# An fp32 two-block transformer on one core: the first block of each feed-forward stage as eight plain products, post-norms spread over two stages

## The chip, the cores and the metric

One NeuronCore of a Trainium2 chip runs the whole program. The time is device microseconds of one execution. All tensors are fp32; batch 1, 512 tokens, width 1024.

## What is computed

Two blocks, each with two layers, on `x` of 512 x 1024. Cut to what matters here:

```python
# first block, per layer: h = h + mixer(rms(h)); h = h + swiglu(rms(h))
def swiglu(h, wg, wu, wd):
    return (silu(h @ wg) * (h @ wu)) @ wd            # 1024 -> 2816 -> 1024
# layer 0's mixer: gated linear attention + stick-breaking attention
# layer 1's mixer: conformer convolution (1024 -> 2048, gate, 31 taps, layer norm, 1024 -> 1024)

# second block, per layer: x = x + rms(mixer(rms(x)), post); x = x + rms(mlp(rms(x)), post)
def sq_relu_mlp(x, w_up, w_down):
    return square(relu(x @ w_up)) @ w_down            # 1024 -> 4096 -> 1024
# layer 0's mixer: differential attention;  layer 1's: short gated convolution (1024 -> 3072, 3 taps)
```

So there are four feed-forward stages: two gated ones (swiglu) and two MLPs. In the second block every mixer and every MLP ends in a post-norm: its whole output must be squared and summed before it can be scaled and added to the residual.

## The kernel before, in words

The residual `res` is held transposed, eight tiles of 128 features x 512 tokens. Every matrix product is made of three fp32r matmuls (`mm3`, lines 296 to 299): each operand is split into a high part (ScalarE copy to fp32r) and a remainder (VectorE subtraction). For weights `w_parts` (L267 to L274) does that: a ScalarE copy into `wh`, a VectorE subtraction at L273 into `wl`; there are four buffers of each, of 128 x 1024. Raw weights come over SyncE's queue into three buffers of 1 MB. For the residual `split_x` (L389) does it, with VectorE at L391. A row scale, one over the root mean square, is applied after the products, because it is a factor per token: `bc_rstd` (L380) squares the eight residual tiles on ScalarE, adds five on GpSimd and three on VectorE (both L373), sums over features by two fp32 matmuls with a tile of ones (L383, L384) and takes Ln and Exp on ScalarE.

The up-projections of the feed-forward stages (`group_s`, L451) compute blocks of 512 output columns with seven products of half-size matrices in place of eight: the features, the columns and the tokens are each cut in two, and a product is 24 matmuls of 256 tokens (L468 to L472). For that it needs sums of weight quarters (VectorE, L480, L492, L493, L507), sums of products (L498, L501, L505), and sums of the activations: for the first four feature tiles the difference of the two token halves (`split_s3`, L413), written over the second half of `xh` and `xl`, and for each pair of tiles three sum tiles (`split_sums`, L420 to L428) in `ph_so`. There are 38 such blocks: 11 in each gated stage and 8 in each MLP. In the first block of a stage one product is put earlier (`first`).

The down-projection and the other projections are plain (`group`, L303, and `out_proj`, L751): four PSUM banks of 128 features x 512 tokens, two passes of 512 features each. Where a post-norm follows, the last weight chunk of the second pass is run in two token halves, and `after_half` is called behind each of them. `Post` (L970) does the post-norm: `evac_last` (L987) takes a finished tile out of PSUM (in the MLP by two VectorE operations, L993 and L994, in the attention by a ScalarE copy), squares it on ScalarE and adds it up on GpSimd (L984). `half` (L1013) makes the matmul with ones (L1016), Ln and Exp, and then `apply` for the tiles: a VectorE scale (L1006), an add to the residual on GpSimd for the tiles 0 to 3 and on VectorE for the others (both L1007), the split, and at a feed-forward stage the differences and sums. Behind it the next stage begins with its `bc_rstd`. At the end of the program `store` transposes the residual back (L1283), copies it out of PSUM (L1285) and writes it (L1286), token half by token half.

What sets the order of instructions on each engine is a scheduler that runs while the program is built. It goes by program order among what is ready, by its own estimate of the times; on the chip every engine follows that order. Two kinds of PSUM tile have four banks each: `mm` for the projections, `at` for the rest.

Of the kernel before, what the change touches and what calls it, by code (L numbers as in the profile page):

```python
# [17 lines left out]
P = 128  # L18
# [91 lines left out]
def body(ctx: ExitStack, tc: tile.TileContext, A, out, consts):  # L110
# [192 lines left out]
    def group(chunks, outs, hs, ls, evac, k_outer=False, halves=(), after_half=None):  # L303
# [6 lines left out]
        for ci, ch in enumerate(chunks):  # L310
# [3 lines left out]
            for tr in trs:  # L314
                ix = [(o, k) for k in range(nk) for o in range(len(outs))] if k_outer else [
                    (o, k) for o in range(len(outs)) for k in range(nk)]
                for o, k in ix:
                    c, m = outs[o]
                    mm3(pss[o][:m, tr], wh[k][:, c : c + m], wl[k][:, c : c + m], hs[kk + k][:, tr], ls[kk + k][:, tr],
# [3 lines left out]
                if after_half and ci == last:  # L323
                    after_half(trs.index(tr))
            kk += nk

    def group_nat(chunks, n, hs, ls, evac, k_outer=False):
# [4 lines left out]
        for ci, ch in enumerate(chunks):  # L332
# [4 lines left out]
            for t, k in ix:  # L337
                ts_ = slice(t * P, (t + 1) * P)
                ps = pss[t][:, :n]
                pe.matmul(ps, hs[kk + k][:, ts_], wh[k], start=ci == 0 and k == 0, stop=False)  # L340
# [90 lines left out]
    def split_s(o, gname, gi):  # L431

        if o < 4:
            split_x(o, V(gname, gi * 8 + o), T0)
            split_s3(o, V(gname, gi * 8 + o))
        else:
            split_x(o, V(gname, gi * 8 + o))
            split_sums(o - 4, V(gname, gi * 8 + o - 4), V(gname, gi * 8 + o))

    def split_s_half(k, gname, gi, i):  # L440

        g = V(gname, gi * 8 + k)
        if i == 0 or k >= 4:
            split_x(k, g, HALVES[i])
        if i == 1:
            if k < 4:
                split_s3(k, g)
            else:
                split_sums(k - 4, V(gname, gi * 8 + k - 4), g)

    def group_s(w0, w1, evac, first=False):  # L451


        bb = []
        for kh in range(2):
# [6 lines left out]
            else:  # L462
                for n, (ap, c) in enumerate((w0, w1)):
                    sync.dma_start(rv[:, :, n * 256 : (n + 1) * 256], ap[rows, c : c + 256].rearrange("(k p) c -> p k c", p=P))
            bb += [rv[:, :, :256], rv[:, :, 256:]]
# [19 lines left out]

        if first:
            product(d, parts(b21), xs(4, T0), True)
# [11 lines left out]
        evac(1, 0, u2)  # L499
        product(a, parts(b12), xs(0, T1))  # L500
        dve.tensor_add(p5, a, p5)  # L501
        evac(1, 1, p5)
        if not first:
            product(d, parts(b21), xs(4, T0), True)
        dve.tensor_add(p1, d, p1)  # L505
        evac(0, 0, p1)
        dve.tensor_add(b21, b21, b22)  # L507
        product(a, parts(b21), xs(4, T1))
        evac(0, 1, a)
# [257 lines left out]
    def add_res_sums(gname, gi):  # L767
        def f(o, ps, tr):
            dve.tensor_add(res[o], res[o], ps)
            split_s(o, gname, gi)  # L770
        return f
# [549 lines left out]
```

## Time and profile before

| | us |
|---|---|
| median of three runs | 2486.16 (2483.38 to 2489.35) |
| the profiled execution | 2486.35 |
| its span, first to last instruction | 2484.5 |
| TensorE busy | 2362.6 |
| VectorE busy | 1620.5 |
| ScalarE busy | 1186.9 |
| GpSimd busy | 233.7 |
| mean granted TensorE clock | 0.978 |

Engines in the profile: PE is TensorE's matmuls, PEld its weight loads, DVE VectorE, ACT ScalarE, POOL GpSimd, SP SyncE. "L273" is line 273 of the kernel. An arrow names what ended a wait. PEclk is the granted TensorE clock as a share of full speed. Matmul records overlap, since the engine is pipelined; how fast it goes is read from how many stand in a stretch. The stages lie in the span, in us and roughly, as follows: attention of the first block to 302, first gated stage to 640, conformer convolution to 900, second gated stage to 1240, differential attention to 1517, first MLP to 1889, short convolution to 2089, second MLP to the end.

### The profile page before, as it was taken

What the parts mean: (1) busy time and instruction counts of PE and PEld (TensorE: products, weight loads), DVE (VectorE), ACT (ScalarE), POOL (GpSimd) and SP (SyncE); (2) the same over time, 40 slices, a digit from 0 to 9 for tenths busy, and PEclk for the clock granted to TensorE, in tenths of its full rate; (3) what the DMA queues carried; (4) which work ended last, traced back from release to release, by engine and by line L of the source; (5) the groups of instructions that cost most, each with busy time, mean ns of one, the idle gap of its engine ahead of it and who ended that gap; (6) DMA issues with size and microseconds to landing.
All of it is one profiled execution on the core that took longest, in us unless ns stands there. A gap on an engine that the chain in (4) does not pass through costs nothing. (4 is left out here: it accounts for less than half of the span.)

```text
span 2484.5 us, 33155 instructions
## 1 busy us (share of the span) xinstructions
PE 2362.6 (95%) x13550; PEld 2008.3 (81%) x13550; DVE 1620.5 (65%) x2096; ACT 1186.9 (48%) x1966; POOL 233.7 (9%) x212
## 2 busy tenths in 40 slices
PE   8999999999998799999999996999998996999997
PEld 6677788989786589898977775898897885898996
DVE  4344795858699787685746767665566545755565
ACT  4663553535654354343434555663354224653552
POOL 0000001010103100202100003000004103000002
PEclk9999999999999899999999998999999998999998
DMA  5112133332312114242331110332332231322420
GB/s 162 35 51 68 51 102 102 103 102 94 111 34 68 34 53 135 68 136 68 128 99 56 51 52 18 122 101 84 102 119 68 85 102 35 102 85 89 132 85 34
DMA packets 148105, 206.84 MB, mean 83 GB/s; under 512 B 5822, under 2 KB 88305, under 8 KB 147953
## 3 DMA queue, kind: packets, MB, share of 16 engines
q1 hardware_dynamic: 147921, 204.72, 25.6%
q8 instruction: 106, 1.74, 0.3%
q14 instruction: 46, 0.38, 0.0%
q10 hardware_dynamic: 32, 0.01, 0.0%
HBM read 202.61 MB, written 2.10 MB: 82 GB/s over the span
## 5 line engine op out<-in xcount | busy, mean ns | idle before, releaser
L297 PE MATMUL ps<-rs,wh 128*128 128x512 f32 (+1 forms) x2976 | 1028.9, 346 | 9.1 <-ACT rs L102 8.2
L298 PE MATMUL ps<-rs,wh 128*128 128x512 f32 (+1 forms) x2976 | 1028.8, 346 | 5.4 <-DVE rs L391 5.4
L299 PE MATMUL ps<-rs,wl 128*128 128x512 f32 (+1 forms) x2976 | 1024.5, 344 | 2.4 <-DVE wl L273 2.4
L273 DVE TENSOR_TENSOR wl<-wraw,wh 128x1024 fp32r<-128x1024 f32 x500 | 606.7, 1221 | 513.3 <-ACT wh L102 512.5
L102 ACT ACTIVATE wh<-wraw 128x1024 fp32r<-128x1024 f32 x500 | 519.7, 1047 | 682.7 <-PE ps L298 553.0
L297 PEld LDWEIGHTS ps<-rs,wh 128*128 128x128 f32 x2976 | 563.7, 190 | 87.1 <-ACT rs L102 11.0
L298 PEld LDWEIGHTS ps<-rs,wh 128*128 128x128 f32 x2976 | 564.1, 190 | 84.1 <-DVE rs L391 7.0
L299 PEld LDWEIGHTS ps<-rs,wl 128*128 128x128 f32 x2976 | 563.6, 189 | 76.8 <-DVE wl L273 2.8
L297 PE MATMUL ps<-ph_so,wh 128*128 128x256 f32 x912 | 260.0, 285 | 5.0 <-ACT fs L102 3.4
L299 PE MATMUL ps<-ph_so,wl 128*128 128x256 f32 x912 | 259.5, 285 | 3.6 <-DVE wl L273 2.4
L298 PE MATMUL ps<-ph_so,wh 128*128 128x256 f32 x912 | 258.6, 284 | 0.7 <-DVE ph_so L396 0.7
L102 ACT ACTIVATE fs<-fs 128x512 f32<-128x512 f32 (+2 forms) x368 | 208.5, 574 | 86.4 <-DVE fs L994 34.5
L297 PEld LDWEIGHTS ps<-ph_so,wh 128*128 128x128 f32 x912 | 175.1, 192 | 7.5 <-ACT fs L102 4.8
L299 PEld LDWEIGHTS ps<-ph_so,wl 128*128 128x128 f32 x912 | 174.9, 192 | 7.7 <-DVE wl L273 7.5
L102 ACT ACTIVATE fs<-ps 128x512 f32<-128x512 f32 (+1 forms) x207 | 116.3, 564 | 129.2 <-PE ps L299 100.5
L298 PEld LDWEIGHTS ps<-ph_so,wh 128*128 128x128 f32 x912 | 175.2, 192 | 1.7 <-DVE ph_so L396 0.9
L102 ACT ACTIVATE rs<-fs 128x512 fp32r<-128x512 f32 (+1 forms) x148 | 91.7, 623 | 78.5 <-DVE fs L800 44.1
L984 POOL TENSOR_TENSOR fs<-fs,fs 128x256 f32<-128x256 f32 (+1 forms) x44 | 46.6, 1058 | 744.4 <-ACT fs L102 737.6
L396 DVE TENSOR_TENSOR rs<-fs,rs 128x512 fp32r<-128x512 f32 x133 | 91.0, 689 | 19.2 <-ACT rs L102 18.8
L812 POOL TENSOR_TENSOR fs<-fs,fs 128x512 f32<-128x512 f32 x32 | 52.2, 1632 | 481.9 <-DVE fs L810 481.9
L102 ACT ACTIVATE rs<-fs,vec 128x256 fp32r<-128x256 f32 (+1 forms) x92 | 52.6, 587 | 67.7 <-DVE fs L814 17.0
L373 POOL TENSOR_TENSOR fs<-fs,fs 128x512 f32<-128x512 f32 x28 | 42.3, 1510 | 342.7 <-ACT fs L102 336.8
(280 smaller groups left out, 2198.6 us busy)
## 6 DMA issues: line engine op xcount, KB each, us to landing
wraw<-in_mlp_w_up_dram SPq DMA_DIRECT2D x32, 1024.0 KB
wraw<-in_mlp_w_down_dram SPq DMA_DIRECT2D x32, 1024.0 KB
wraw<-in_ffn_w_up_dram SPq DMA_DIRECT2D x44, 512.0 KB
wraw<-in_ffn_w_gate_dram SPq DMA_DIRECT2D x44, 512.0 KB
wraw<-in_ffn_w_down_dram SPq DMA_DIRECT2D x20, 1024.0 KB
wraw<-in_cv_w_pw_dram SPq DMA_DIRECT2D x16, 512.0 KB
wraw<-in_attn_w_qkv_dram SPq DMA_DIRECT2D x16, 512.0 KB
wraw<-in_conv_w_in_dram SPq DMA_DIRECT2D x16, 512.0 KB
```

The lines of the kernel that those rows point to most:

```text
L102: r = self.engine.activation(out, in_, func, **kw)
L273: dve.tensor_sub(v(wl), src, v(b(wh)))
L297: pe.matmul(ps, wh, h, start=start, stop=False, skip_group_check=True)
L298: pe.matmul(ps, wh, l, start=False, stop=False, skip_group_check=True)
L299: pe.matmul(ps, wl, h, start=False, stop=stop, skip_group_check=True)
L373: r = eng.tensor_add(acc, acc, s)
L396: dve.tensor_sub(l, src, b(h))
L812: pool_e.tensor_add(res[o], res[o], s)
L984: pool_e.tensor_add(self.acc[:, tr], self.acc[:, tr], s[:, tr])
```

## The change

Four things change.

1. The first block of each of the four feed-forward stages runs all eight block products by `group_plain`, one token half after the other: the k-tiles outside, four column tiles inside, 96 matmuls of 256 tokens for a half. It needs no sums. The tiles of sums and differences for the later blocks are made during it and after it (`split_all_sums`, then `split_s3`).
2. `Post` no longer works per half behind the projection. `steps` is called after each output tile of the second token half: after the second, the statistics of the first half and two of its tiles, then one, then five. The second half's statistics and tiles (`second`) come from within the next stage: behind k = 1 of the first half of the plain block, or of the short convolution's first group. The adds on GpSimd are those of the tiles 1, 3 and 5.
3. The short convolution's first group (`group_first`) runs wholly in token halves, where before its first weight chunk did. The row scales (`bc_rstd`) come later: in the gated stages behind k = 3 of the plain block's first half, in the MLPs behind the plain block, in the short convolution behind k = 5 of the group's second half, in the conformer convolution and the attention ahead of the last k of the first group.
4. At the end, the second half's statistics come ahead of the first half's store.

The diff, cut to its core (the signatures follow):

```diff
+    def group_first(chunks, outs, hs, ls, evac, at):
+        pss = [bank() for _ in outs]
+        ws = [load_w(*ch) for ch in chunks]
+        nk = chunks[0][2]
+        for i, tr in enumerate(HALVES):
+            for k in range(2 * nk):
+                wh, wl = (w[k % nk] for w in ws[k // nk])
+                for o, (c, m) in enumerate(outs):
+                    mm3(pss[o][:m, tr], wh[:, c : c + m], wl[:, c : c + m], hs[k][:, tr], ls[k][:, tr],
+                        i == 0 and k == 0, i == 1 and k == 2 * nk - 1)
+                if (i, k) in at:
+                    at[i, k]()
+        for o, (c, m) in enumerate(outs):
+            evac(o, pss[o][:m], None)
...
+    def group_plain(w0, w1, evac, at):
+        ws = []
+        for rv in load_blocks(w0, w1):
+            for h in range(2):
+                wh, wl = w_parts(rv[:, 2 * h : 2 * h + 2, :].rearrange("p k c -> p (k c)"), 1024)
+                ws += [(wh[:, k * T : (k + 1) * T], wl[:, k * T : (k + 1) * T]) for k in range(2)]
+        for th, tr in enumerate((T0, T1)):
+            pss = [bank(), bank()]
+            for k in range(8):
+                for n in range(2):
+                    for p in range(2):
+                        wh, wl = (t[:, n * 256 + p * P : n * 256 + (p + 1) * P] for t in ws[k])
+                        mm3(pss[n][:, p * 256 : (p + 1) * 256], wh, wl, xh[k][:, tr], xl[k][:, tr], k == 0 and p == 0, k == 7)
+                if (th, k) in at:
+                    at[th, k]()
+            for n in (1, 0):
+                evac(n, th, pss[n], False)
...
-                group_s((wu, col), (wg, col), evac, pi == 0 and fc == 0)
+                if pi == 0 and fc == 0:
+                    group_plain((wu, col), (wg, col), evac, {(0, 3): norm, (1, 0): lambda: split_all_sums("ffnn", layer)})
+                    after_first()
+                else:
+                    group_s((wu, col), (wg, col), evac)
...
+                (pool_e if k in (1, 3, 5) else dve).tensor_add(res[k][:, x], res[k][:, x], m[:, x])
...
+        def steps(self, n):
+            if n == 2:
+                self.stats(0)
+            ks = {2: range(0, 2), 3: range(2, 3), 4: range(3, 8)}.get(n)
+            if ks:
+                self.apply(ks, 0)
+
+        def second(self):
+            self.stats(1)
+            self.apply(range(8), 1)
+            self.free()
...
-                group_s((wu, f0 * P), (wu, f0 * P + 256), evac, pi == 0 and g == 0)
+                if pi == 0 and g == 0:
+                    group_plain((wu, f0 * P), (wu, f0 * P + 256), evac, {
+                        (0, 1): before.second, (1, 0): lambda: split_all_sums("fpre", layer)})
+                    for k in range(4):
+                        split_s3(k, V("fpre", layer * 8 + k))
+                    rb, acc = bc_rstd(res)
+                    freeF(acc)
+                    dve.tensor_mul(rb, rb, rb)
+                    post = Post().then("fpost", layer, nxt)
+                else:
+                    group_s((wu, f0 * P), (wu, f0 * P + 256), evac)
...
+            group_first(ch, outs, xh, xl, cv_evac, {(0, 1): post.second, (1, 5): cv_norm})
...
-    mlp(1, None, store)
+    post = mlp(1, None, post)
+    post.stats(1)
+    store(0)
+    post.apply(range(8), 1)
+    store(1)
+    post.free()
```

## Rows read from the trace of the kernel before

**Rows 1.** The page's first section: busy us, share of the span, instructions

```profile
PE 2362.6 (95%) x13550; PEld 2008.3 (81%) x13550; DVE 1620.5 (65%) x2096; ACT 1186.9 (48%) x1966; POOL 233.7 (9%) x212
```

**Rows 2.** Stretches; columns: us, busy us and instructions by engine, PEclk, DMA share, GB/s

```profile
298.00:340.00 42.00, 35.86 (x248) 32.31 (x247) 39.43 (x55) 28.47 (x43) 1.52 (x1) 0.96 0.16 51
655.00:685.00 30.00, 28.81 (x122) 22.51 (x121) 24.19 (x36) 25.58 (x61) 2.06 (x1) 1.00 0.33 106
900.00:980.00 80.00, 75.35 (x609) 72.90 (x609) 70.15 (x81) 44.55 (x59) 0.00 (x0) 1.00 0.31 99
1240.00:1260.00 20.00, 19.15 (x89) 14.88 (x88) 16.27 (x26) 11.04 (x17) 1.95 (x2) 1.00 0.35 117
1517.60:1588.40 70.80, 46.10 (x343) 42.65 (x344) 65.33 (x95) 49.50 (x85) 12.02 (x12) 0.83 0.21 69
1878.00:1926.00 48.00, 37.84 (x221) 32.45 (x220) 36.48 (x53) 21.67 (x39) 23.05 (x20) 0.89 0.21 66
2088.60:2159.60 71.00, 46.62 (x343) 43.43 (x343) 65.42 (x95) 49.41 (x85) 12.11 (x12) 0.81 0.21 67
2453.00:2484.50 31.50, 16.60 (x87) 12.24 (x85) 19.93 (x39) 6.21 (x14) 11.49 (x14) 0.70 0.18 67
1600.00:1620.00 20.00, 20.00 (x87) 16.09 (x86) 3.76 (x4) 4.65 (x7) 0.00 (x0) 1.00 0.34 106
1640.00:1660.00 20.00, 20.00 (x172) 20.00 (x171) 17.71 (x19) 15.81 (x23) 0.00 (x0) 1.00 0.33 106
1513.40:1566.00 52.60, 28.16 (x197) 24.87 (x196) 50.65 (x81) 33.39 (x65) 15.82 (x16) 0.77 0.11 37
```

**Rows 3.** Groups by line, 1513.4 to 1566: busy us, mean ns, idle before

```profile
L273 DVE TENSOR_TENSOR wl<-wraw,wh 128x1024 fp32r<-128x1024 f32 x6 | 7.3, 1218 | 1.3 <-ACT wh L102 1.3
L383 PE MATMUL ps<-fs,ones 128*128 128x512 f32 x2 | 2.1, 1142 | 18.2 <-POOL fs L373 18.2
L1016 PE MATMUL ps<-fs,ones 128*128 128x256 f32 x2 | 1.2, 714 | 4.7 <-POOL fs L984 4.7
L384 PE MATMUL ps<-fs,ones 128*128 128x512 f32 x2 | 1.1, 644 | 0.4 <-DVE fs L373 0.4
```

**Rows 4.** Timeline, 2100 to 2135, GpSimd and VectorE: start us, us

```profile
2112.95 2.79 POOL L373 TENSOR_TENSOR fs<-fs,fs 128x512 f32<-128x512 f32 x2 [1.75 <-ACT fs L102]
...
2114.55 1.48 DVE L1007 TENSOR_TENSOR fs<-fs,fs 128x256 f32<-128x256 f32 x1
...
2118.47 0.41 DVE L1007 TENSOR_TENSOR fs<-fs,fs 128x256 f32<-128x256 f32 x1
2118.80 0.48 DVE L425 SCALAR_TENSOR_TENSOR fs<-fs,vec,fs 128x256 f32<-128x256 f32 x1
2119.20 0.68 DVE L373 TENSOR_TENSOR fs<-fs,fs 128x512 f32<-128x512 f32 x1
```

**Rows 5.** Timeline, 1500 to 1592, TensorE and VectorE

```profile
1511.62 0.70 PE L1016 MATMUL ps<-fs,ones 128*128 128x256 f32 x2 [0.61 <-POOL fs L984]
...
1513.45 3.13 DVE L1006 SCALAR_TENSOR_TENSOR fs<-fs,vec,fs 128x256 f32<-128x256 f32 x4 [4.52 <-ACT fs L102]
...
1587.98 0.39 PE L297 MATMUL ps<-rs,wh 128*128 128x512 f32 x1
```

**Rows 6.** Groups by line, 1513.4 to 1566, GpSimd

```profile
L1007 POOL TENSOR_TENSOR fs<-fs,fs 128x256 f32<-128x256 f32 x8 | 7.1, 906 | 5.5 <-DVE fs L1006 5.5
L373 POOL TENSOR_TENSOR fs<-fs,fs 128x512 f32<-128x512 f32 x4 | 5.5, 1380 | 4.9 <-ACT fs L102 4.8
L984 POOL TENSOR_TENSOR fs<-fs,fs 128x256 f32<-128x256 f32 x4 | 3.3, 827 | 6.9 <-ACT fs L102 6.9
```

**Rows 7.** Timeline of the end of the span

```profile
2456.26 0.70 PE L1016 MATMUL ps<-fs,ones 128*128 128x256 f32 x2 [1.20 <-POOL fs L984]
...
2470.01 1.22 PE L1016 MATMUL ps<-fs,ones 128*128 128x256 f32 x2 [2.66 <-POOL fs L984]
2472.22 4.33 DVE L1006 SCALAR_TENSOR_TENSOR fs<-fs,vec,fs 128x256 f32<-128x256 f32 x6 [3.88 <-ACT fs L102]
```

More of the change, by code (lines that the diff above doesn't have):

```diff
@@ L301, in body, with group @@
     HALVES = (slice(0, 256), slice(256, 512))
-    def group(chunks, outs, hs, ls, evac, k_outer=False, halves=(), after_half=None):
+    def group(chunks, outs, hs, ls, evac, k_outer=False, halves=(), steps=None, late=None):
         pss = [bank() for _ in outs]
@@ L318, in group @@
                     c, m = outs[o]
+                    if late and ci == last and k == nk - 1 and o == 0:
+                        late()
                     mm3(pss[o][:m, tr], wh[k][:, c : c + m], wl[k][:, c : c + m], hs[kk + k][:, tr], ls[kk + k][:, tr],
@@ L339, in group_nat @@
                 ps = pss[t][:, :n]
+                if late and ci == last and k == nk - 1 and t == 0:
+                    late()
                 pe.matmul(ps, hs[kk + k][:, ts_], wh[k], start=ci == 0 and k == 0, stop=False)
@@ L1017, in half, with apply, free @@
             rsqrt_ln(self.rm[:, tr], pb[:, :256], 1.0 / D)
-            _, _, nxt, each = self.args
-            for k in range(4 if nxt and not self.sums else 8):
-                self.apply(k, tr)
-            if each:
-                each(i)
-        def finish(self):
-            if self.args[2] and not self.sums:
-                for k in range(4, 8):
-                    self.apply(k, slice(0, T))
+        def apply(self, ks, i):
+            gname, gi, nxt = self.args
+            x = HALVES[i]
+            for k in ks:
+                m = self.m[k]
+                dve.scalar_tensor_tensor(m[:, x], m[:, x], V(gname, gi * 8 + k), self.rm[:, x], ALU.mult, ALU.mult)
+                (pool_e if k in (1, 3, 5) else dve).tensor_add(res[k][:, x], res[k][:, x], m[:, x])
+                if nxt:
+                    split_x(k, V(nxt[0], nxt[1] * 8 + k), x)
+        def steps(self, n):
[8 more added lines that the diff above has]
+            self.free()
+        def free(self):
             freeF(self.rm, self.m, self.acc)
@@ L1055, in body @@
     dve.tensor_scalar(gsub, V("subln"), 1.0 - lam_init, None, ALU.mult)
-    rb, acc = bc_rstd(res)
-    pr = bank("at")
-    for t in range(NT):
-        for i in range(2):
-            pe.matmul(pr[:, t : t + 1], acc[i][:, t * P : (t + 1) * P], ones[:, 0:1], start=i == 0, stop=i == 1, skip_group_check=True)
     rn2 = cpool.tile([P, NT], F32, name="rn2")
-    rsqrt_ln(rn2, pr[:, :NT], 1.0 / D)
-    freeF(acc)
     sync.dma_start(*const_tiles(["dmask", "rot", "cosr", "sinr"]))
@@ L1069, in body, with da_norm @@
     cosb, sinb = C["cosr"], C["sinr"]
-    dve.tensor_mul(cosb, cosb, rb)
-    dve.tensor_mul(sinb, sinb, rb)
-    freeF(rb)
+    def da_norm():
+        rb, acc = bc_rstd(res)
+        pr = bank("at")
+        for t in range(NT):
+            for i in range(2):
+                pe.matmul(pr[:, t : t + 1], acc[i][:, t * P : (t + 1) * P], ones[:, 0:1], start=i == 0, stop=i == 1, skip_group_check=True)
+        rsqrt_ln(rn2, pr[:, :NT], 1.0 / D)
+        freeF(acc)
+        dve.tensor_mul(cosb, cosb, rb)
+        dve.tensor_mul(sinb, sinb, rb)
+        freeF(rb)
     wqkv = A["attn_w_qkv_2"][0]
@@ L1270, in body @@
     freeF(rb, rb2)
-    post = Post().then("mpost", 1, ("fpre", 1), sums=True)
+    post = Post().then("mpost", 1, ("fpre", 1))
     out_proj(A["conv_w_out_2"][0], 0, 8, hh, hl, lambda o, ps, tr: post.evac_last(o, ps, tr), halves=True,
-             after_half=post.half)
+             steps=post.steps)
     freeR(hh, hl)
-    post.finish()
     def store(i):
```

148 lines of the change are left out of this document (66 added, 82 removed).

## The prediction, before the run

> **What bounds the kernel now.** I read the page's first section, then cut the span into stretches, then asked in the bad stretches what TensorE waits for. TensorE is busy for 2362.6 of 2484.5 us [rows 1], so 122 us are idle and the rest can only be shortened by less work. The stretches [rows 2] say where the idle time lies. Inside a stage TensorE does not rest: 172 matmuls of 256 columns in 20 us (0.116 us each) and 87 of 512 columns in 20 us (0.230 us each). At the seams it does: 6.1 us idle at the first gated stage (298 to 340), 4.6 at the second (900 to 980), 24.7 and 24.4 at the two MLP stages, 10.2 at the short convolution, 14.9 at the end, 1.2 at the conformer convolution and 0.9 at the attention. That is 87 us.
>
> At an MLP seam the granted clock averages 0.83 and 0.81, so lost time is more than idle time there. Of the 70.8 us after the out-projection, the 336 matmuls of the first two blocks need 39.1 us at 0.116, and L1016, L383 and L384 4.4 [rows 3]; **27 us** are lost.
>
> What ends those waits: TensorE stands 18.2 us at L383 for GpSimd's L373, after 4.7 us at L1016 [rows 3]. GpSimd is only the last in line. VectorE is busy for 50.65 of the 52.6 us from 1513.4 on, GpSimd for 15.82 [rows 2]: the seam is a **VectorE queue** of post-norm, split, difference and sum tiles, into which L383 waits.
>
> **VectorE's prices.** Back to back, a fused operation on 256 columns starts 0.40 us before the next one, an add 0.33; each record is 0.08 longer than that, so a 512-column add (0.68) counts 0.60 [rows 4] and a weight remainder of 1024 columns (1.22) 1.14 [rows 3]. The stretch's 81 instructions are 44 fused ones, 16 adds of 256 columns, 12 of 512 and 9 of 1024: 17.6 + 5.3 + 7.2 + 10.3 = 40.4 us. The other 10.3 are delay beside GpSimd: L1007 takes 0.41 alone and 1.48 while GpSimd's L373 runs [rows 4]. So 65% of GpSimd's 15.82 us came on top.
>
> The Trainium skill, SBUF — State Buffer, "Who interferes with whom", says that a VectorE instruction with two SBUF inputs and a GpSimd instruction that reads SBUF exclude each other and the loser fully blocks. The single 1.48 us instance agrees; the stretch's 65% is below it. What it would give is a rival below.
>
> **The change, part by part.**
>
> *Eight products for seven, four times.* 192 matmuls replace 168; 24 x 0.116 = 2.8 us of TensorE each, **11.2 in all**. Nothing hides it where TensorE is the bound.
>
> *First block's VectorE work.* Seven remainders, four weight sums and three product sums become four remainders: 3 x 1.14 + 4 x 1.14 + 3 x 0.60 = 9.8 us less, two weight sums of which ran before the queue begins now.
>
> *MLP stages.* Now the first statistics matmul stands after the first half with an idle wait of 0.61, and VectorE starts at 1513.45 [rows 5]. Afterwards it stands behind two outputs of the second half (24 matmuls, 2.8 us), so VectorE starts about 1.9 us later, at 1515.3; TensorE no longer waits. From there, before the second block's two first products can run, VectorE has: first-half apply 8 x 0.40 + 5 x 0.33 + 8 x 0.40 = 8.05 (three adds go to GpSimd, four now); second half the same; two remainders 2.3; four evacuations 2.4; sums tiles 4 x (3 x 0.40 + 0.60 + 0.33) = 8.5; difference tiles 4 x 0.73 = 2.9; square adds and the squared scale 1.8; two remainders and a weight sum of the second block 3.4. Sum: 37.4. GpSimd runs 6 x 0.91 + 4 x 1.38 + 4 x 0.83 = 14.3 us [rows 6]; at 65%, 9.3. So the second block's second product starts at 1515.3 + 46.7 = 1562.0, its first could start 2.8 earlier, 1559.2. Now the second block, counted back from the first 512-column matmul at 1587.98 [rows 5] by 168 x 0.116, effectively starts at 1568.5: 9.3 us gained. If the differences and the squared scale (3.5 us, needed only later in that block) slip behind, 12.8. I take **11 per stage, 22**. TensorE's own bound would be 27 - 2.8 = 24 per stage, reached only if VectorE's queue stayed hidden; it sits nearer 11, because 37 us of work stand against 22.3 us of plain block. The low end is 4, with full exclusion. L383 now waits behind the plain block (192 matmuls, 22.3 us); its chain needs the second-half adds, ready about then, so I cost it nothing beyond VectorE's queue. If its squares come late, it holds the second block up, in the same gap.
>
> *Gated stages.* The residual is complete before the block, the splits are full width, and only four sums and differences (11.4 us) plus 4.2 of evacuation and some 7 of remainders and adds are queued beside 22.3 us of plain block. L383 stands at k = 3, 5.6 us in; the gate evacuations that need its result wait until the half ends at 11. First stage: 6.1 - 2.8 - 0.7 left over = **+2.6** (bounds -1 to +3). Second: 4.6 - 2.8 - 0.8 = **+1** (-2 to +2).
>
> *Short convolution.* 256-column pairs for one 512-column matmul cost 2 x 0.116 against 0.230, nothing to 0.3 us. VectorE's apply (16.1), remainders (2.3) and GpSimd's delay fill the 22.3 us of the first group, so the halves pace closely; then L383 at k = 5 of the second half holds what follows it, and the first evacuation waits for its Ln, Exp and square, an estimated 3 to 4 us in which the next group has no bank. Of 10.2 us some 6 remain: **+4.5** (bounds 0 and 9).
>
> *Conformer and attention.* L383 moves into the group's last step: **+1** and **+0.8**, the idle now shown. Row scales come later by a microsecond or two: the bounds are -2 each and +1.2, +0.9. The constant load on SP's queue and the two GpSimd copies behind it now precede the sums; some 22 us of group cover them.
>
> *End.* Now the second statistics matmul waits until 2470.01 for squares that ran behind output copies, and VectorE's last apply starts at 2472.22 [rows 7]. Afterwards those statistics are asked for before the stores. The first ones can run at 2456.26, when their squares are there now [rows 7]; 24 matmuls later, at 2459.5, the half ends; two adds, a square and a GpSimd add put the last square near 2462.7, and the second apply follows the first on VectorE, at about 2465.7 (an estimate). **+6.5** (bounds 3 and 9); then adds, transposes, copies and stores as now. DMA counts do not change: each first block loads two weight tiles, released earlier as no weight is rewritten.
>
> **Sum.** 22 + 2.6 + 1 + 4.5 + 1 + 0.8 + 6.5 = 38.4, which already has the 11.2 in it. The profiled execution took 2486.35 us, 0.2 over the median of 2486.16: 2486.35 - 38.4 = **2448 us**.
>
> **Rivals.**
> 1. *VectorE's queue stays hidden*, the seams go to TensorE's bound: MLP 24 each, short convolution 8: gain 68, **2418**. For it: all of that work has the whole plain block to run in. Against: 46.7 us in 22.3 of cover. 0.15.
> 2. *VectorE is held for all of GpSimd's time*: 14.3 instead of 9.3 per MLP stage takes 5 off each gain, the short convolution keeps 1, the end 3.5: 12 + 2.6 + 1 + 1 + 1.8 + 3.5 = 22, **2464**. For it: the 1.48 us instance; against: the 65%. 0.17. This is what the rule of the Trainium skill's SBUF — State Buffer would do.
> 3. *The matmuls' order does not follow*: it is settled when the program is built, so L383 could stand where it stands now, the 27 us stay and the eighth product is added: 38.4 - 22 - 5.6 = 11, **2475**. 0.05.
> 4. *Slower: the plain block holds all four weight buffers* (wh, wl) until late in its second half, and the second block's weights are converted behind evacuations and difference tiles that wait for that half's end. At the first MLP seam VectorE idles 1.3 us for such weights [rows 3]; the rival decides where each of the four stages has 38.4 / 4 = 9.6 us of added gap. At 12: 2448 + 48 = **2496**. For it: VectorE runs in a fixed order; against: two of the buffers are free from k = 3 of the second half, 5.6 us before its end. 0.08.
>
> **Numbers.** The forecast has 0.55, its own range 2437 to 2460 (MLP 8 to 15, short convolution 1 to 7). To leave out no more than 2 in 10, I reach over rivals 2 and 3, and downward to just short of rival 1: 2421 to 2478. Within 0.2% (5 us, about what a measurement of this kernel can tell from no change) lie the edges of rivals 3 and 4: 0.05. Slower: the rest of rival 4, 0.07. Faster: 0.88.
>
> **What would show it.** Right: 24 more matmuls at each of four stages; waits at L1016 near nothing; TensorE's idle at each MLP seam down to 10 to 16 us, with VectorE over 90% busy until the second block's second product; a last apply near 2435 to 2440 in a shorter span. Rival 1 shows VectorE with gaps in the plain block; rival 2 VectorE operations at 1 us and more beside each GpSimd add; rival 3 a wait of 18 us at L383 again; rival 4 TensorE idle after the last plain matmul at all four stages with the remainder waiting for its weight. A gated stage that idles more than 3 us, or L383 ending more than 5 us of wait in the short convolution, makes that term wrong.

## The result, and the profile after

The changed kernel takes 2451.18 us (median of four runs, 2448.55 to 2452.56) against 2486.49 for the kernel before beside it: a ratio of 0.9857 with an interval of 0.984 to 0.9874. It is faster by 35.3 us; 38.4 were forecast, a time of 2448. The profiled execution took 2451.22 us. The page's first section, against [rows 1], shows the 144 matmuls added (96 for four products, 48 for the short convolution's pairs) and 9.6 us more TensorE time in a span 35 us shorter:

```profile
PE 2372.2 (97%) x13694; PEld 2023.2 (83%) x13694; DVE 1587.3 (65%) x2084; ACT 1175.0 (48%) x1954; POOL 224.4 (9%) x204
```

**Where it came from.** I divided both spans at the places where TensorE changes from 512-column to 256-column matmuls or back, read from the timelines; the same places exist in every kernel here. A "seam" runs from such a change to the stage's first down-projection. Lengths in us (gains are rounded after subtracting):

| stretch | before | after | gain | forecast |
|---|---|---|---|---|
| start, to the first gated seam | 302.6 | 306.8 | -4.2 | 0 |
| first gated seam | 91.3 | 85.7 | 5.5 | 2.6 |
| from its last down-projection through the conformer convolution | 270.1 | 268.5 | 1.6 | 1 |
| second gated seam | 88.3 | 84.7 | 3.6 | 1 |
| from its last down-projection through the attention | 289.6 | 288.3 | 1.3 | 0.8 |
| first MLP seam | 84.0 | 76.4 | 7.6 | 11 |
| short convolution | 199.1 | 191.4 | 7.7 | 4.5 |
| second MLP seam | 84.2 | 76.5 | 7.8 | 11 |
| end, from the last 256-column half | 37.1 | 32.9 | 4.2 | 6.5 |

The stretches not listed (three down-projections and blocks between them in each stage) agree to 0.1 us each. Outside the start the gain is 39.3 us, so the forecast's 38.4 is nearly met, by terms that are off in both directions. The start gave 4.2 back in this pair of profiles, though up to 268 us the order of the instructions is the same in both kernels. The windows from 100 to 150 us, of before and of after (start:end, length, busy us and instructions by engine, PEclk, DMA share, GB/s):

```profile
100.00:150.00 50.00, 50.00 (x231) 34.98 (x230) 18.50 (x32) 32.83 (x65) 0.52 (x1) 0.97 0.14 43
```

```profile
100.00:150.00 50.00, 50.00 (x208) 34.31 (x208) 17.28 (x29) 29.89 (x60) 0.52 (x1) 0.90 0.13 42
```

TensorE is busy for all 50 us in both, yet gets through 208 matmuls in place of 231, at a granted clock of 0.90 in place of 0.97. Over the twelve profiles of this study the start lasts from 299.8 to 306.8 us; the last experiment below, with the changed kernel's own order on every engine, has 303.3. The kernel before varies as well: beside the first two sets of experiments it took 2488.87 and 2489.71 us. So single runs are read by their stretches, not by their totals. Of the variants below, the first was run four times and the parts put together five times; the others were run once. Where a variant leaves the MLP seams as they are, these take 76.4 to 77.2 us, so less than 1 us in one seam is no finding.

**The seams after**, answering to [rows 2] in its order, each window moved with its stage: the two gated stages, the first MLP, the short convolution, the second MLP, the end. The seventh is 20 us inside the first MLP's seam; the eighth is the gap in it.

```profile
302.20:344.20 42.00, 41.44 (x319) 39.22 (x318) 35.93 (x53) 27.59 (x43) 1.30 (x1) 1.00 0.20 62
897.10:977.10 80.00, 79.78 (x661) 78.37 (x661) 69.53 (x86) 46.41 (x62) 0.00 (x0) 1.00 0.31 99
1509.80:1572.80 63.00, 49.50 (x366) 46.20 (x367) 58.86 (x92) 43.66 (x79) 12.63 (x10) 0.86 0.18 59
1862.60:1910.60 48.00, 43.30 (x302) 39.37 (x301) 45.31 (x77) 23.60 (x44) 17.42 (x19) 0.96 0.21 67
2065.50:2128.80 63.30, 50.11 (x366) 46.81 (x367) 59.12 (x93) 43.80 (x79) 12.81 (x10) 0.87 0.18 59
2422.10:2449.40 27.30, 16.88 (x87) 12.87 (x85) 20.93 (x41) 6.33 (x14) 9.56 (x12) 0.69 0.21 77
1520.00:1540.00 20.00, 15.48 (x132) 15.27 (x131) 20.00 (x39) 15.09 (x32) 8.86 (x7) 0.95 0.17 53
1535.20:1549.90 14.70, 3.46 (x8) 1.17 (x6) 14.22 (x21) 9.60 (x19) 5.55 (x4) 0.60 0.00 0
```

The gated stages hardly idle any more (0.6 and 0.2 us). Each MLP seam idles 13.5 and 13.2 us where it idled 24.7 and 24.4. VectorE is busy for all of the 20 us from 1520 on, which reach 4.8 us into the gap, and for 14.22 of 14.70 us in the gap.

What stands where L383 stood 18.2 us in [rows 3]: the row scale's two matmuls with ones are now L406 and L407, and the square adds L396. Groups by line, 1509.8 to 1572.8 (busy us, mean ns, idle before and its releaser):

```profile
L396 POOL TENSOR_TENSOR fs<-fs,fs 128x512 f32<-128x512 f32 x4 | 7.2, 1791 | 7.6 <-ACT fs L102 7.4
...
L406 PE MATMUL ps<-fs,ones 128*128 128x512 f32 x2 | 2.1, 1142 | 5.6 <-POOL fs L396 5.6
L407 PE MATMUL ps<-fs,ones 128*128 128x512 f32 x2 | 2.1, 1142 | 5.7 <-DVE fs L396 5.7
```

The gap in the timeline of TensorE: the plain block's last matmul, the two waits, the first matmuls of the second block's first and second products.

```profile
1535.20 0.28 PE L299 MATMUL ps<-rs,wl 128*128 128x256 f32 x1
1541.04 2.08 PE L406 MATMUL ps<-fs,ones 128*128 128x512 f32 x2 [5.56 <-POOL fs L396]
1548.79 2.08 PE L407 MATMUL ps<-fs,ones 128*128 128x512 f32 x2 [5.68 <-DVE fs L396]
1549.88 1.20 PE L297 MATMUL ps<-rs,wh 128*128 128x256 f32 x1
...
1553.97 0.28 PE L297 MATMUL ps<-ph_so,wh 128*128 128x256 f32 x1
```

What VectorE and GpSimd do meanwhile, from the timeline of all engines:

```profile
1533.59 7.40 POOL L396 TENSOR_TENSOR fs<-fs,fs 128x512 f32<-128x512 f32 x4 [7.38 <-ACT fs L102]
1533.96 0.48 DVE L447 SCALAR_TENSOR_TENSOR fs<-fs,vec,fs 128x256 f32<-128x256 f32 x1
1534.35 1.02 DVE L419 TENSOR_TENSOR ph_so<-fs,ph_so 128x512 fp32r<-128x512 f32 x2
1535.29 1.50 DVE L448 SCALAR_TENSOR_TENSOR fs<-fs,vec,fs 128x256 f32<-128x256 f32 x1
1536.71 1.75 DVE L419 TENSOR_TENSOR ph_so<-fs,ph_so 128x512 fp32r<-128x512 f32 x1
...
1538.38 1.48 DVE L446 SCALAR_TENSOR_TENSOR fs<-fs,vec,fs 128x256 f32<-128x256 f32 x1
1539.79 1.48 DVE L419 TENSOR_TENSOR ph_so<-fs,ph_so 128x256 fp32r<-128x256 f32 x1
...
1541.59 0.47 DVE L440 SCALAR_TENSOR_TENSOR rs<-fs,vec,rs 128x256 fp32r<-128x256 f32 x1
...
1547.25 1.49 DVE L396 TENSOR_TENSOR fs<-fs,fs 128x512 f32<-128x512 f32 x2 [0.27 <-ACT fs L102]
1548.72 1.22 DVE L273 TENSOR_TENSOR wl<-wraw,wh 128x1024 fp32r<-128x1024 f32 x1
```

While GpSimd's four adds run, four VectorE instructions take 1.50, 1.75, 1.48 and 1.48 where 0.48, 0.68, 0.48 and 0.41 are the usual durations: 4.2 us lost. The row of 7.40 us merges four adds, which singly last 2.92, 1.33, 1.59 and 1.32 us: in the first 1.8 us of the long one VectorE's instructions keep their usual durations, and from then on theirs are the long ones. The differences (L440) for the later blocks stand ahead of VectorE's share of the square adds (L396), and the second block's first weights (L273) stand behind all of it.

The end, against [rows 7]: both statistics matmuls (now L1047), VectorE's output copies (L1349) and the start of the second apply (L1055).

```profile
2425.38 0.70 PE L1047 MATMUL ps<-fs,ones 128*128 128x256 f32 x2
...
2433.48 1.22 PE L1047 MATMUL ps<-fs,ones 128*128 128x256 f32 x2 [0.39 <-POOL fs L1026]
```

```profile
2435.23 0.74 DVE L1056 TENSOR_TENSOR fs<-fs,fs 128x256 f32<-128x256 f32 x2
2435.90 1.27 DVE L1349 COPY fs<-ps 128x512 f32<-128x512 f32 x2
2437.10 0.86 DVE L1055 SCALAR_TENSOR_TENSOR fs<-fs,vec,fs 128x256 f32<-128x256 f32 x2
```

### The profile page after: what moved, and what is told of

Read it like the earlier page. It is cut to its first block, busy times and chain, and to the rows that moved or that the text cites. A ratio compares the mean times of both kernels' runs of the same rounds, so it can differ in the third digit from the quotient of the medians.

```text
span 2449.4 us, 33423 instructions
## 1 busy us (share of the span) xinstructions
PE 2372.2 (97%) x13694; PEld 2023.2 (83%) x13694; DVE 1587.3 (65%) x2084; ACT 1175.0 (48%) x1954; POOL 224.4 (9%) x204
## 3 DMA queue, kind: packets, MB, share of 16 engines
q8 instruction: 107, 1.75, 0.3%
## 5 line engine op out<-in xcount | busy, mean ns | idle before, releaser
L297 PE MATMUL ps<-rs,wh 128*128 128x512 f32 (+1 forms) x3120 | 1069.1, 343 | 12.3 <-ACT rs L102 10.7
L298 PE MATMUL ps<-rs,wh 128*128 128x512 f32 (+1 forms) x3120 | 1066.1, 342 | 5.5 <-DVE rs L414 5.5
L299 PE MATMUL ps<-rs,wl 128*128 128x512 f32 (+1 forms) x3120 | 1064.9, 341 | 2.3 <-DVE wl L273 2.3
L273 DVE TENSOR_TENSOR wl<-wraw,wh 128x1024 fp32r<-128x1024 f32 (+1 forms) x488 | 591.5, 1219 | 507.7 <-ACT wh L102 506.9
L102 ACT ACTIVATE wh<-wraw 128x1024 fp32r<-128x1024 f32 (+1 forms) x488 | 508.4, 1047 | 685.1 <-PE ps L298 546.8
L297 PEld LDWEIGHTS ps<-rs,wh 128*128 128x128 f32 x3120 | 591.5, 190 | 89.6 <-ACT rs L102 13.1
L298 PEld LDWEIGHTS ps<-rs,wh 128*128 128x128 f32 x3120 | 592.5, 190 | 82.5 <-DVE rs L414 6.8
L299 PEld LDWEIGHTS ps<-rs,wl 128*128 128x128 f32 x3120 | 592.2, 190 | 75.0 <-DVE wl L273 2.7
L299 PE MATMUL ps<-ph_so,wl 128*128 128x256 f32 x816 | 232.2, 285 | 1.5
L297 PE MATMUL ps<-ph_so,wh 128*128 128x256 f32 x816 | 231.0, 283 | 1.7 <-ACT wh L102 1.7
L298 PE MATMUL ps<-ph_so,wh 128*128 128x256 f32 x816 | 230.7, 283 | 0.0
L299 PEld LDWEIGHTS ps<-ph_so,wl 128*128 128x128 f32 x816 | 156.3, 192 | 4.3 <-DVE wl L273 4.3
L297 PEld LDWEIGHTS ps<-ph_so,wh 128*128 128x128 f32 x816 | 156.4, 192 | 2.5 <-ACT wh L102 2.1
L298 PEld LDWEIGHTS ps<-ph_so,wh 128*128 128x128 f32 x816 | 156.3, 192 | 0.0
L1026 POOL TENSOR_TENSOR fs<-fs,fs 128x256 f32<-128x256 f32 (+1 forms) x44 | 42.9, 976 | 708.0 <-ACT fs L102 700.9
L396 POOL TENSOR_TENSOR fs<-fs,fs 128x512 f32<-128x512 f32 x28 | 43.9, 1568 | 348.1 <-ACT fs L102 335.9
```

The costliest lines, as they stand in the source:

```text
L102: r = self.engine.activation(out, in_, func, **kw)
L273: dve.tensor_sub(v(wl), src, v(b(wh)))
L297: pe.matmul(ps, wh, h, start=start, stop=False, skip_group_check=True)
L298: pe.matmul(ps, wh, l, start=False, stop=False, skip_group_check=True)
L299: pe.matmul(ps, wl, h, start=False, stop=stop, skip_group_check=True)
L396: r = eng.tensor_add(acc, acc, s)
```

## The experiments

My theory of the changed kernel: an MLP seam is still held by the order in which the row scale is asked for. Its square adds and its two matmuls with ones stand ahead of the second block's products, though its result is needed only later. Rivals: VectorE simply has too much work for the cover it is given; or GpSimd's adds hold VectorE up. Every edit is against the changed kernel. Stretches are named as in the table above; lengths in us:

| kernel | start | 1st gated | 2nd gated | 1st MLP | its first down-projection | short conv. | 2nd MLP | end |
|---|---|---|---|---|---|---|---|---|
| changed kernel | 306.8 | 85.7 | 84.7 | 76.4 | 45.0 | 191.4 | 76.5 | 32.9 |
| scale late | 306.3 | 86.0 | 85.0 | 77.0 | 46.3 | 191.5 | 75.2 | 32.9 |
| scale late, tied | 305.1 | 85.9 | 84.9 | 70.1 | 46.3 | 191.5 | 70.2 | 32.9 |
| squares on VectorE | 305.2 | 85.5 | 84.7 | 75.0 | 45.0 | 191.5 | 74.3 | 32.9 |
| post-norm adds on VectorE | 302.5 | 85.7 | 84.7 | 75.6 | 45.0 | 190.5 | 74.6 | 32.2 |
| two plain blocks | 305.6 | 88.9 | 87.9 | 69.1 | 45.4 | 191.5 | 67.8 | 32.9 |
| two plain, tied, adds on VectorE | 303.2 | 85.7 | 84.9 | 62.7 | 46.3 | 190.8 | 62.4 | 32.1 |
| gated stages as before | 304.2 | 91.7 | 88.5 | 76.9 | 45.0 | 191.4 | 76.9 | 32.9 |
| short convolution as before | 299.8 | 85.5 | 85.2 | 77.1 | 45.0 | 197.9 | 77.2 | 32.9 |

**The row scale asked for behind the first down-projection.**

```diff
-                    rb, acc = bc_rstd(res)
-                    freeF(acc)
-                    dve.tensor_mul(rb, rb, rb)
                     post = Post().then("fpost", layer, nxt)
...
             out_proj(wd, pi * 8, 8, hh, hl, part_evac, halves=pi == 3, steps=post.steps if pi == 3 else None)
             freeR(hh, hl)
+            if pi == 0:
+                rb, acc = bc_rstd(res)
+                freeF(acc)
+                dve.tensor_mul(rb, rb, rb)
```

> The changed kernel with one move: in both MLPs the row scale (its squares, GpSimd adds, L406, L407 and the squared scale) comes behind the first down-projection in place of behind the plain block. In the changed kernel each MLP seam leaves TensorE 5.6 us waiting at L406 and 5.7 at L407. Theory A, VectorE's queue with GpSimd's holds ends the seam: what leaves the queue there is two square adds and the squared scale (about 2 us) and the 4.4 us by which four VectorE operations beside GpSimd's adds run longer than alone, so some 6.5 us per MLP and 2451 - 13 = 2438. Theory B, the two waits in TensorE's order are the whole loss: 11.3 per MLP, 2428. Theory C, the sum and difference tiles and the second block's weights end it alone: 0 to 2 per MLP, 2447 to 2451.

Measured: 2450.49 us (2449.77 to 2454.71), a ratio to before of 0.9843 (0.9826 to 0.986): no gain on the changed kernel. The waits at L406 and L407 are gone from the seam, but TensorE waits for a weight remainder instead. GpSimd and VectorE in the timeline of all engines:

```profile
1544.37 8.28 POOL L396 TENSOR_TENSOR fs<-fs,fs 128x512 f32<-128x512 f32 x4 [16.54 <-ACT fs L102]
1545.43 2.19 DVE L514 TENSOR_TENSOR wraw<-wraw 128x1024 f32<-128x1024 f32 x1
...
1545.45 0.58 PE L299 MATMUL ps<-rs,wl 128*128 128x256 f32 x1 [7.92 <-DVE wl L273]
...
1547.65 2.20 DVE L523 TENSOR_TENSOR wraw<-wraw,wraw 128x1024 f32<-128x1024 f32 x1
1549.78 1.75 DVE L396 TENSOR_TENSOR fs<-fs,fs 128x512 f32<-128x512 f32 x1
1551.45 3.42 DVE L273 TENSOR_TENSOR wl<-wraw,wh 128x1024 fp32r<-128x1024 f32 x2
1553.78 0.58 PE L299 MATMUL ps<-ph_so,wl 128*128 128x256 f32 x1 [3.93 <-DVE wl L273]
```

The squares are ready early, and the scheduler put them back into the gap, beside the second block's weight work, which they stretch (2.19 for a sum of 1.23). The edit moved the matmuls and left the adds, so the theory was not yet tried.

**The same, with the squares tied** behind the down-projection's first output by an order-only dependency.

```diff
-    def sumsq(tiles):
+    def sumsq(tiles, after=None):
...
                 else:
                     s = F()
-                    act.activation(s, tiles[i], AF.Square)
+                    q = act.activation(s, tiles[i], AF.Square)
+                if after:
+                    tc.add_manual_dep(q.ins, after, order)
...
+            if pi == 0:
+                rb, acc = bc_rstd(res, mark[0])
```

> As e1_scale_late, but the eight squares on ScalarE are tied in order behind the first evacuation of the first down-projection, so that they, GpSimd's adds and L396 really leave the seam. In e1 they had come back into it: beside GpSimd's four adds L514 and L523 took 2.2 us each in place of 1.2, a pair of L273 3.4 in place of 2.4, and L396 1.75. Theory A, VectorE's queue with GpSimd's holds ends the seam: those 4.9 us per MLP go against e1, so the stretch from the out-projection's half to the first down-projection falls from 77.0 and 75.2 us to some 72 and 70. Theory C, the sum and difference tiles and the second block's weights end it alone: the stretches stay within 1 us of e1's.

Measured: 2440.49 us. The seams fall to 70.1 and 70.2, by 6.3 and 6.2; the first down-projection that now holds the scale grows from 45.0 to 46.3, and the block behind it takes 0.5 more. That is 4.4 us net per stage, which includes what GpSimd's adds take from VectorE (the next run). TensorE's largest wait in the seam is one weight remainder (L274 here is L273 with one line added; engine, line, releaser: us in total, times, longest):

```profile
PE ps L300 <- DVE wl L274: 8.6, 2, 8.2
PE ps L299 <- DVE rs L418: 1.7, 1, 1.7
```

So the row scale's place costs 4.4 us per stage, and behind it VectorE's queue still holds the second block for 8.

**The squares added on VectorE**, none on GpSimd, in the place where the change has them.

```diff
-    def sumsq(tiles):
+    def sumsq(tiles, pool=pool_e):
...
-        for eng, ix in ((pool_e, range(0, 5)), (dve, range(5, 8))):
+        for eng, ix in ((pool, range(0, 5)), (dve, range(5, 8))):
...
-                    rb, acc = bc_rstd(res)
+                    rb, acc = bc_rstd(res, dve)
```

> The four adds for the MLP's row scale, 1.85 us each on GpSimd, go to VectorE (about 0.6 us each); everything else as in the changed kernel. Read by the MLP stretches (76.4 and 76.5 us in the changed kernel), since the stretch before the first gated stage varies by some microseconds from run to run. Theory A: GpSimd's four adds held VectorE for 4.4 us in this seam (full exclusion by the two 512-column adds), so VectorE gets 4.4 back, pays 2.4, and the matmul with ones no longer waits for GpSimd's last add: the stretches go to about 74.4, the total to about 2447. Theory B: VectorE is little disturbed by GpSimd and its queue is simply long, so the four adds lengthen it: about 78.8 per stretch, total about 2456. Theory C: the wait for the row scale (5.6 + 5.7 us in front of the two matmuls with ones) is what costs, not VectorE's queue; without GpSimd's chain it falls away and the stretches go to about 71, total about 2440.

Measured: 2446.3 us, seams of 75.0 and 74.3, 1.4 and 2.1 less than in the changed kernel, about theory A's 2. VectorE's instructions of the gap keep their short durations (0.41 to 0.69). The second block's weights come up behind these adds, and TensorE now waits 9.2 us for the first of them. The timeline of all engines:

```profile
1541.79 3.09 DVE L396 TENSOR_TENSOR fs<-fs,fs 128x512 f32<-128x512 f32 x5
1543.21 0.58 PE L297 MATMUL ps<-rs,wh 128*128 128x256 f32 x1 [9.25 <-ACT wh L102]
1544.80 1.21 DVE L273 TENSOR_TENSOR wl<-wraw,wh 128x1024 fp32r<-128x1024 f32 x1
1544.93 2.08 PE L406 MATMUL ps<-fs,ones 128*128 128x512 f32 x2 [0.92 <-DVE fs L396]
```

Four adds of 0.62 us on VectorE cost less than the 4.2 us that GpSimd took from it. The waits for the row scale are nearly gone, but they don't take 11 us with them: theory C is refuted, since another wait ends last in their place.

**The post-norm's adds on VectorE.**

```diff
-                (pool_e if k in (1, 3, 5) else dve).tensor_add(res[k][:, x], res[k][:, x], m[:, x])
+                dve.tensor_add(res[k][:, x], res[k][:, x], m[:, x])
```

> The changed kernel with all residual adds of the post-norm on VectorE, none on GpSimd. Per MLP seam VectorE gets six adds more (6 x 0.33 = 2.0 us) and GpSimd loses six of 0.91 (5.4 us). Theory A at 65%: 3.5 us of delay go, 1.5 gained per MLP seam and as much at the short convolution: 2451 - 4.5 = 2446. Full exclusion: 3.4 gained per seam, 2441. No interference: 2 lost per seam, 2457.

Measured: 2442.16 us. By stretches the gain is 0.7 and 1.9 at the MLPs, 0.9 at the short convolution, 0.7 at the end, and 0.7 at the conformer convolution, where nothing was edited, so each is good to about as much. At the three places of the theory that is 3.5 us, where 65% made it 4.5 and full exclusion 10: nearer to 65%.

**Two plain blocks per stage.**

```diff
-                if pi == 0 and fc == 0:
-                    group_plain((wu, col), (wg, col), evac, {(0, 3): norm, (1, 0): lambda: split_all_sums("ffnn", layer)})
-                    after_first()
+                if pi == 0 and fc < 2:
+                    group_plain((wu, col), (wg, col), evac, {} if fc else {(0, 3): norm, (1, 0): lambda: split_all_sums("ffnn", layer)})
+                    if fc:
+                        after_first()
...
-                if pi == 0 and g == 0:
+                if pi == 0:
+                    group_plain((wu, f0 * P), (wu, f0 * P + 256), evac, {} if g else {
                         (0, 1): before.second, (1, 0): lambda: split_all_sums("fpre", layer)})
+                    if g == 0:
+                        continue
```

> The changed kernel with the second block of each of the four stages plain as well; sums as now, differences and (in the MLPs) the row scale behind the second block. TensorE gets 24 matmuls more per stage, 2.8 us. Theory A, VectorE's queue ends the MLP seams: the second plain block needs no sum tiles and gives the queue 22 us more of cover, so the 14.7 us between the first block's last and the second's first matmul close and each MLP gains about 10 to 12; the gated stages, which TensorE bounds, lose 2.8 each: 2451 - 22 + 5.6 = 2435. Theory B, waits at L406 and L407 alone: they move behind the second block and shrink, with the same sign. If the seams were already at TensorE's bound: 4 x 2.8 = 11.2 lost, 2462.

Measured: 2441.6 us. Each gated seam grows by 3.2: that is what one more eighth product costs there, where 24 x 0.116 had made it 2.8. The MLP seams fall by 7.3 and 8.7, and 0.4 of that goes to the down-projection behind each. If they pay the same price, another 22 us of cover took 10.5 and 11.9 us off TensorE's path. This run doesn't part VectorE's queue from the row scale, which moved with it.

**The parts put together**: a second plain block in the MLPs alone, the tied row scale, and the post-norm's adds on VectorE.

```diff
+                if pi == 0:
+                    group_plain((wu, f0 * P), (wu, f0 * P + 256), evac, {} if g else {
                         (0, 1): before.second, (1, 0): lambda: split_all_sums("fpre", layer)})
+                    if g == 0:
+                        continue
...
+                rb, acc = bc_rstd(res, mark[0])
...
+                dve.tensor_add(res[k][:, x], res[k][:, x], m[:, x])
```

> A version put together from the runs: two plain blocks in the MLPs alone (they cost 3.2 us a stage where TensorE is the bound and gave 7.3 and 8.7 in the MLPs), the residual adds of the post-norm all on VectorE (some 4 us in all), the row scale tied into the first down-projection. If the parts add up: 2451 - 16 - 4 = 2431, and some 1 to 3 us less for the scale. If VectorE's queue is hidden already by the second plain block, the last two parts give nothing: 2435. If the adds on VectorE and the splits no longer fit beside the first plain block: 2440.

Measured: 2425.58 us (2423.2 to 2428.71), a ratio to before of 0.9748 (0.9734 to 0.9761), where the changed kernel has 0.9857. It beats both kernels. Between the two profiles (2423.2 us here) lie 28.0 us, 3.6 of them in the start, where nothing was edited. What is left of TensorE's waits in the first MLP seam, and the window of it (3.9 us idle at a granted clock of 1.00, where the changed kernel's whole seam, 1496.1 to 1572.5, has 14.8 at 0.89):

```profile
PE ps L300 <- DVE wl L274: 1.9, 1, 1.9
PE ps L298 <- ACT rs L102: 0.9, 1, 0.9
PE ps L299 <- DVE rs L418: 0.7, 1, 0.7
```

```profile
1494.00:1556.30 62.30, 58.45 (x483) 57.47 (x483) 46.63 (x93) 40.71 (x81) 6.79 (x8) 1.00 0.25 78
```

**The gated stages as before**, seven products in their first block and the row scale in its old place; `split_s` is put back.

```diff
+        norm()
...
-                if pi == 0 and fc == 0:
-                    group_plain((wu, col), (wg, col), evac, {(0, 3): norm, (1, 0): lambda: split_all_sums("ffnn", layer)})
-                    after_first()
-                else:
-                    group_s((wu, col), (wg, col), evac)
+                group_s((wu, col), (wg, col), evac, pi == 0 and fc == 0)
...
```

> The changed kernel with the two gated stages as before the change: seven products in the first block, row scale ahead of it, sums and differences from the tile evacuations. By the forecast's terms 2.6 + 1 = 3.6 us come back, 2455. By the lengths of the stages in the two traces (first 5.5, second 3.7 shorter) 9.2 come back, 2460; TensorE then waits again at the row scale's second matmul for VectorE's square adds, about 4 us, in the first gated stage.

Measured: 2460.08 us; the two seams go back to 91.7 and 88.5, within 0.4 of before. The wait at the row scale's second matmul is there again:

```profile
PE ps L407 <- DVE fs L396: 4.0, 1, 4.0
```

So the gated gains are real, 5.9 and 3.8 us by this run, and larger than the forecast's.

**The short convolution's norms ahead of its first group**, which runs in halves only in its first chunk again.

```diff
+    post.second()
+    cv_norm()
...
-            group_first(ch, outs, xh, xl, cv_evac, {(0, 1): post.second, (1, 5): cv_norm})
+            group(ch, outs, xh, xl, cv_evac, True, (0,))
```

> The changed kernel with the short convolution's seam as before: second half of the post-norm and row scale ahead of the first group, only the first weight chunk in token halves. By the forecast 4.5 us come back, by the two traces' lengths 7.7 (199.1 us against 191.4 from the MLP's last halves to the out-projection's): 2455.5 or 2459. If the steps after each output alone made the gain there: 2451.

Measured: 2452.83 us, with the shortest start of all, 299.8. The stretch is 197.9, 6.5 more than in the changed kernel: of its gain of 7.7, 6.5 come from the first group in halves with the norms inside it (not parted here), the rest from the post-norm's steps or from what such stretches vary by. TensorE's waits from 1850 to 1930:

```profile
PE ps L298 <- DVE rs L414: 3.0, 4, 1.4
PE ps L297 <- ACT rs L102: 2.7, 3, 1.6
PE ps L406 <- POOL fs L396: 2.7, 1, 2.7
PE ps L1047 <- POOL fs L1026: 1.1, 1, 1.1
```

**The conformer's and the attention's row scale ahead of their first group.**

```diff
+    conv_norm()
     w1 = A["cv_w_pw1"][0]
...
-                      xh, xl, lambda o, ps, tr: pw1_evac(2 * j + o, ps, tr), j == 0, late=None if j else conv_norm)
+                      xh, xl, lambda o, ps, tr: pw1_evac(2 * j + o, ps, tr), j == 0, late=None)
...
+    da_norm()
     wqkv = A["attn_w_qkv_2"][0]
...
-        group_nat(k_chunks([(wqkv, 2 * D + c * T, 2 * D + (c + 1) * T)], 0, 8), T, xh, xl, v_evac, c == 0, None if c else da_norm)
+        group_nat(k_chunks([(wqkv, 2 * D + c * T, 2 * D + (c + 1) * T)], 0, 8), T, xh, xl, v_evac, c == 0)
```

> The changed kernel with the row scales of the conformer convolution and the attention ahead of their first group again. By the forecast 1.8 us come back, by the two traces' lengths 2.9 (1.6 in the conformer stretch, 1.3 in the attention's): 2453 to 2454, with TensorE waiting about 1 us at L406 at each place. If the gain there came from elsewhere: 2451.

Measured: 2452.55 us. The attention's stretch grows from 288.3 to 290.1, with 1.4 us of wait at L406 back, as the theory has it. The conformer's is 268.4 against 268.5, although 0.6 us of wait at L406 came back, and where nothing in it was edited it takes 267.8 to 269.2. So the conformer's 1.6 is not shown to come from the moved row scale.

**At the end, the store asked for ahead of the second statistics.**

```diff
     post = mlp(1, None, post)
-    post.stats(1)
     store(0)
+    post.stats(1)
     post.apply(range(8), 1)
```

> Only the order of the end: the first half's store is asked for ahead of the second half's statistics, as the kernel before had it. Read by the stretch from the last half's first matmul to the end (37.1 us before, 32.9 in the changed kernel). Theory A, that of the prediction: the gain of the end comes from the statistics standing before the stores; it goes back to 36 to 37 us. Theory B: the gain comes from the statistics and tiles of the first half now being put into the second half's matmuls, and the order of statistics and stores is worth little: 33 to 34 us. Theory C: the output copies that ran in front of the second apply go still further forward and the transfer of the first half starts earlier, so the end is not longer or even shorter: 31 to 33 us.

Measured: 2447.95 us, an end of 32.9 as in the changed kernel. The instructions of every engine come out in the same order: the scheduler takes the statistics when their squares are there, wherever the program puts them. So this run is one more run of the changed kernel, and the written order of statistics and stores is worth nothing. What is left for the gain of the end is the steps of the post-norm inside the projection, and three adds on GpSimd where there were four; neither was tried alone.

## Why the prediction was right, and where its terms were off

The forecast of 2448 us and its range held. **Its mechanism held too**: at each of the four stages 24 more matmuls, waits at the first statistics gone, VectorE over 90% busy through the plain block, and at the MLPs a remaining gap of the order forecast (13.5 us idle, 10 to 16 named). Rival 1 did not come, since VectorE has no gaps in the plain block. Rival 3 did not come as drawn; the 18.2 us at L383 became 5.6 and 5.7. Rival 4 did not come: the gated stages idle 0.6 and 0.2 us. Its picture fits the MLPs in part, where the second block's first weights are converted last, at 1547.6 and 1548.7.

That the total is so near is in part luck: the MLPs and the end fell 8.9 us short of their terms and the start lost 4.2, while the other places gave 9.8 more than theirs. No run undoes the change in the MLPs. That their 15.4 us come from the plain block and the spread post-norm rests on the two traces, and how much each of the two gives is not shown. The terms:

- **MLP stages, 11 forecast, 7.6 and 7.8 measured: the largest miss.** The sum of VectorE's queue was the sound part, and it gave 9.3. It put the second block's second product at 1562.0; that starts at 1553.97 in a seam that begins 7.8 us earlier, so at 1561.8 on the old scale. What fell short came behind it: 144 matmuls at 0.116 would take 16.7 us, and 18.6 pass, 1.0 of them in a wait for a weight copy. I went up from 9.3 to 11 because the differences and the squared scale might slip behind; only the squared scale did (L1275 at 1555.00). The matmul with ones, of which I said "I cost it nothing beyond VectorE's queue", was no miss beside that sum; but its place inside the queue costs 4.4 us net per stage, as tying the squares shows, and moving GpSimd's adds to VectorE alone gives 1.4 and 2.1.
- **Rival 2, full exclusion.** I gave the forecast GpSimd's time at 65%. By instance, what the Trainium skill's SBUF — State Buffer, "Who interferes with whom", says shows plainly: VectorE instructions of two SBUF inputs take 1.48 to 1.75 us beside GpSimd's adds. By stretch VectorE loses 4.2 of GpSimd's 7.40 us, 57%, since others of the same kind run at 0.48 inside it, while GpSimd's first add takes 2.92 in place of some 1.33. Taking GpSimd's adds away gave 3.5 us for the post-norm's at the three places forecast, and 3.5 for the MLPs' squares, after what VectorE pays to do them itself. The forecast's share was the better one, and the time is 2451, not 2464.
- **Gated stages, 2.6 and 1 forecast, 5.5 and 3.6 measured.** The step that failed is "6.1 - 2.8 - 0.7" and "4.6 - 2.8 - 0.8": it set idle time against the product. These seams lost more than they idled (6.4 and 4.7 us over the whole of them). At the steady rate of the later blocks (336 matmuls in 39.8 us, 0.1185 each) and with 2.1 us for the row scale's matmuls with ones, 672 matmuls need 81.7 us; the seams took 91.3 and 88.3, so they lost 9.6 and 6.6. Afterwards 696 need 84.6 against 85.7 and 84.7. I had made this account for the MLPs, where the clock was visibly low, and not here.
- **Short convolution, 4.5 forecast, 7.7 measured.** Again only idle was counted: it goes from 10.2 to 4.7 us, and the granted clock of the window from 0.89 to 0.96. The 3 to 4 us without a bank that I feared behind the row scale were one wait of 1.2 us.
- **Conformer and attention, 1 and 0.8 forecast, 1.6 and 1.3 measured.** The attention's is shown by undoing it (1.8). The conformer's is not: it did not come back with its row scale.
- **End, 6.5 forecast, 4.2 measured.** "Those statistics are asked for before the stores" changed nothing, since the scheduler's order ignores it. The second apply starts 20.6 us behind the half's first matmul where 18.3 were forecast. The first apply lasts from 2427.07 to 2435.90, interleaved with evacuations, then two output copies still go ahead.
- **The start**, costed at nothing, lost 4.2 us between the two profiles at an unchanged order. The medians of both kernels differ by 35.3 us, 4 less than the stretches outside the start, so the loss may not be of this pair of profiles alone; whether the change has a part in it was not tried.

## What to carry to other kernels

Count what a seam loses against the steady rate of the same matmuls, not the idle time of the engine: the gated seams lost 9.6 and 6.6 us where they idled 6.4 and 4.7. Where a helper engine's result is needed late, tie its work behind something late; moving it in program order does not hold a scheduler that takes what is ready. And when a queue of VectorE is longer than its cover, more cover (a second plain block, 3.2 us) can cost less than what it takes off the gap (10 to 12 us).

## What the runs showed of the hardware that was not expected

- **GpSimd and VectorE slow each other, not one the other.** GpSimd's add of 256 columns takes 0.73 to 0.74 us in the changed kernel while VectorE is idle (L1026, 1498.7 to 1506.5) and 0.84 to 0.91 beside it. One of 512 columns takes 1.38 on average in [rows 6], 1.32 to 2.92 among VectorE's sum tiles of the changed kernel (7.40 for four), and 2.07 on average beside weight sums of 1024 columns (8.28 for four). Those sums take 2.19 and 2.20 where 1.23 is usual. So an add of 512 columns cost the VectorE instruction beside it about 1 us, and one of 256 columns about 0.5 (L1055: 0.94 to 0.96 in place of 0.48). An add moved to VectorE costs 0.62 us there.
- **The granted clock also sinks where TensorE's records leave no idle time.** From 100 to 150 us it was 0.97 in one profile and 0.90 in another; between the two levels of 1.2 and 2.4 GHz a mean of 0.90 means a fifth of the stretch at the lower one. TensorE had been busy for all of the 50 us before in both. The start of this program differs with it: its six profiles with a mean clock of 0.97 from 50 to 300 us have starts of 305.1 to 306.8 us, the three with 0.99 starts of 299.8 to 303.2. Why it sinks stays open.
